# The adaLN modulation of a hybrid block by halves of the features, in plain fp32

## The chip, the cores and the metric

The kernel runs on one core of a Trainium2 chip. The metric is the time of one execution on the device, in microseconds. Before the change the median of three runs is 1171.71 us (1171.58 to 1171.74).

## The reference

One layer of a diffusion backbone, all in float32. A conditioning vector `c` and a learned vector `c_ctx` go through SiLU and a matrix `w_ada` [1024 x 6144]; the six sections of the result are shift, scale and gate for two sub-layers. The part at issue is the first use of shift and scale:

```python
mod_x = (silu_c @ w_ada[layer] + b_ada[layer])[:, None, :]
mod_c = silu_cc @ w_ada[layer] + b_ada[layer]
...
px = modulate(rms_norm(x, g_pre_mix[layer]), sh_m, sc_m) @ w_in[layer]
pc = modulate(rms_norm(ctx, g_pre_mix[layer]), csh_m, csc_m) @ w_in[layer]
```

`x` holds 1024 latent tokens and `ctx` 256 context tokens, of 1024 features each. `modulate(h, shift, scale)` is `h * (1 + scale) + shift`. The projections feed windowed attention and a bidirectional chunkwise mLSTM; an output projection and a SwiGLU sub-layer follow. Nothing can be projected before scale and shift are known, and every feature of a token enters each projected value.

## The kernel before

A float32 product of full accuracy is made of three matmuls of a rounded format (`mm3`, lines 77 to 79): each operand is split into a high part (a cast on ScalarE, ACT) and a low part (a subtraction on VectorE, DVE), and high x high, high x low and low x high are summed. A plain fp32 matmul does the same at once, in several passes.

**Head.** The DMA queue on SyncE (SP) takes the loads in a fixed order, each issued behind the one before (`issue_after(last)`). First come the modulation weights of the scale section (1) and the shift section (0), eight loads each of 128 rows x 1024 columns (`wa`, line 315, 512 KB, rows of 4 KB), with the first two token tiles between (`prep_a`, line 192). Six of the sixteen are multiplied in plain fp32 (`PLAIN`), ten are split (lines 65 and 66), and the stationary operand is the SiLU vector, four columns wide (`cz4`, `cs4`; products at line 334). The results `pr`, [4 x 512] twice per section, are copied to rows of `Vc` (ACT at line 355, DVE at 359), eight small transposes put them into columns (`pcol`, line 362), and DVE makes `scol` (scale and gain, lines 366 to 368) and `hcol` (shift, line 371), 128 partitions x 8 feature groups. `w1` (272 columns of `w_in`: gates, attention values and one mLSTM value head) is loaded behind and split at lines 295 and 300.

**Tokens.** There are ten tiles of 128 tokens, 0 to 7 latent and 8 and 9 context. For each of the tiles 0 to 5: load, sum of squares on ACT (line 196), root and reciprocal, scaling of the rows on GpSimd (POOL, line 204), eight transposes on TensorE (PE, line 220) into two PSUM tiles `pt`, one for each half of the features; then multiply by `scol` (line 243), add `hcol` (line 256, from tile 2 on on POOL), cast to the high part `hh` (line 268; 265 for tile 0) and subtract for the low part `hl` (line 269). Tiles 6 to 9 are loaded transposed and use the root as a row of factors. `s1(i)` is the slab of 272 columns: 24 matmuls over eight feature groups of 128 (for tile 0 in another order, lines 391 and 394). `s2(i)` is the slab of 384 columns, with weights `w2` split at lines 460 and 461. Three `s2` slabs (`NFILL = 3`) are put between the `s1` slabs; `gates()`, a chain of small steps on other engines, comes behind `s1(9)`, and the other seven `s2` slabs run on PE meanwhile. Then `tproj` makes 13 token projections (lines 608 to 611), and the rest of the layer follows.

The program is put in order by a scheduler that goes by data dependences and priority; `keep_in_program_order` (`pin` in the changed kernel) fixes an instruction's place among the others so marked, and `issue_after` holds an instruction behind another. Within an engine and within the load queue, instructions then run in the order of the list. Work buffers are `R(k, ...)`, sixteen of 4 KB per partition, where a later tile of the same number waits for the readers of the former.

## Time and profile before

| | |
|---|---|
| median of 3 runs | 1171.71 us (1171.58 to 1171.74) |
| the profiled execution's own time | 1171.69 us |
| its span | 1169.9 us |
| mean granted clock of TensorE | 0.998 |
| busy time | PE 1155.5 us (99%), DVE 782.8, ACT 558.6, POOL 154.5 |
| read from memory, written | 159.29 MB, 55.97 MB |

How to read it: times are from the span's start. A timeline row has start, length, engine, source line, operation, output<-input, tile, shapes, count, and in brackets the idle time before it with what ended it. A row of windows has the stretch, its length, busy time of PE, PE's weight loads, DVE, ACT and POOL with the count of instructions, the clock granted to PE (1.00 is full), the share in which the DMA engines were busy, and GB/s. Matmuls overlap, so the distance of two starts is the cost of one, not its length.

### The profile page before, as it was taken

What the parts mean: (1) busy time and instruction counts of PE and PEld (TensorE: products, weight loads), DVE (VectorE), ACT (ScalarE), POOL (GpSimd) and SP (SyncE); (2) the same over time, 40 slices, a digit from 0 to 9 for tenths busy, and PEclk for the clock granted to TensorE, in tenths of its full rate; (3) what the DMA queues carried; (4) which work ended last, traced back from release to release, by engine and by line L of the source; (5) the groups of instructions that cost most, each with busy time, mean ns of one, the idle gap of its engine ahead of it and who ended that gap; (6) DMA issues with size and microseconds to landing.
All of it is one profiled execution on the core that took longest, in us unless ns stands there. A gap on an engine that the chain in (4) does not pass through costs nothing.

```text
span 1169.9 us, 16222 instructions
## 1 busy us (share of the span) xinstructions
PE 1155.5 (99%) x5857; PEld 945.5 (81%) x5857; DVE 782.8 (67%) x1391; ACT 558.6 (48%) x1037; POOL 154.5 (13%) x201
## 2 busy tenths in 40 slices
PE   9899999999999999999999999999999999999997
PEld 3799888878888767888788888888888888888886
DVE  5874768873787643479777777767677755644557
ACT  6753442223777855877543333334343344434533
POOL 1430001263664630000000000000000000000000
PEclk9999999999999999999999999999999999999999
DMA  9722954657797605220334556566645467665853
GB/s 367 281 68 80 391 175 144 210 170 230 206 254 202 174 10 198 90 83 26 99 135 171 199 206 241 212 201 219 222 143 161 150 212 273 201 208 191 307 181 126
DMA packets 103272, 216.99 MB, mean 185 GB/s; under 512 B 10260, under 2 KB 39572, under 8 KB 101784
## 3 DMA queue, kind: packets, MB, share of 16 engines
q1 hardware_dynamic: 103192, 215.95, 55.5%
q8 instruction: 46, 0.75, 0.3%
q14 instruction: 34, 0.28, 0.1%
HBM read 159.29 MB, written 55.97 MB: 184 GB/s over the span
## 4 chain that ended last, share of the span: by engine, by line
PE 95%; DMA 2%; DVE 2%; issue 0%; ACT 0%; SPq 0%; DVEq 0%
PE xv L79 8%; PE xv L77 8%; PE xv L78 8%; PE pt L78 6%; PE pt L79 6%; PE pt L77 6%; PE t L609 4%; PE t L611 4%; PE t L608 4%; PE pt L1063 3%; PE pt L1045 3%; PE op L77 3%; PE op L78 3%; PE op L79 2%; PE fx L77 2%; PE fx L79 2%
## 5 line engine op out<-in xcount | busy, mean ns | idle before, releaser
L66 DVE TENSOR_TENSOR fo<-fr,fo 128x1024 fp32r<-128x1024 f32 x77 | 92.8, 1223 | 71.4 <-ACT fo L65 69.9
L65 ACT CAST fo<-fr 128x1024 fp32r<-128x1024 f32 x77 | 79.5, 1049 | 74.1 <-PE pt L79 38.2
L608 PE MATMUL t<-hh,th 128*128 128x512 f32 x208 | 82.4, 396 | 0.0
L609 PE MATMUL t<-hl,th 128*128 128x512 f32 x208 | 82.0, 394 | 0.0
L1445 ACT CAST wS<-wr 128x512 fp32r<-128x512 f32 x88 | 54.2, 622 | 55.4 <-PE pt L79 36.8
L1447 DVE TENSOR_TENSOR wS<-wr,wS 128x512 fp32r<-128x512 f32 x88 | 60.4, 689 | 19.7 <-ACT wS L1445 19.7
L79 PE MATMUL xv<-tT,wS 128*128 128x512 f32 x168 | 65.6, 391 | 0.0
L77 PE MATMUL xv<-tT,wS 128*128 128x512 f32 x168 | 65.6, 391 | 0.0
L78 PE MATMUL xv<-tT,wS 128*128 128x512 f32 x168 | 65.5, 390 | 0.0
L611 PE MATMUL t<-hh,tl 128*128 128x512 f32 x208 | 65.0, 393 | 0.0
L77 PE MATMUL op<-woh,mh 128*128 128x512 f32 x128 | 50.9, 397 | 0.0
L79 PE MATMUL op<-woh,ml 128*128 128x512 f32 x128 | 50.0, 390 | 0.0
L78 PE MATMUL op<-wol,mh 128*128 128x512 f32 x128 | 50.0, 390 | 0.0
L1193 DVE TENSOR_TENSOR wr<-wr 128x512 f32<-128x512 f32 x66 | 45.5, 690 | 1.4
L608 PEld LDWEIGHTS t<-hh,th 128*128 128x128 f32 x208 | 39.1, 188 | 8.3 <-issue 0.3
L1479 ACT ACTIVATE es<-es 128x512 f32<-128x512 f32 x22 | 13.9, 633 | 66.6 <-DVE es L1196 66.5
L609 PEld LDWEIGHTS t<-hl,th 128*128 128x128 f32 x208 | 39.1, 188 | 8.0 <-issue 1.2
L77 PE MATMUL pt<-fo 128*128 128x512 f32 x110 | 42.8, 389 | 0.0
L78 PE MATMUL pt<-fo 128*128 128x512 f32 x110 | 42.8, 389 | 0.0
L79 PE MATMUL pt<-fo 128*128 128x512 f32 x110 | 42.8, 389 | 0.0
L611 PEld LDWEIGHTS t<-hh,tl 128*128 128x128 f32 x208 | 37.2, 188 | 6.5 <-issue 0.3
L782 PE MATMUL s<-k,qh 128*128 128x256 f32 (+1 forms) x128 | 41.6, 336 | 0.5 <-DVE sm L784 0.5
(788 smaller groups left out, 3339.3 us busy)
## 6 DMA issues: line engine op xcount, KB each, us to landing
wr<-in_wfi SPq DMA_DIRECT2D x44, 512.0 KB, 5.2
wb<-in_wada SPq DMA_DIRECT2D x24, 512.0 KB, 5.8
s_d<-a SPq DMA_DIRECT2D x22, 512.0 KB, 6.7
bt<-in_wfo SPq DMA_DIRECT2D x44, 256.0 KB, 3.4
tb_d<-bt SPq DMA_DIRECT2D x11, 1024.0 KB, 3.9
fr<-s_d SPq DMA_DIRECT2D x44, 256.0 KB, 4.4
fr<-tb_d SPq DMA_DIRECT2D x44, 256.0 KB, 4.6
fr<-a_d SPq DMA_DIRECT2D x33, 256.0 KB, 4.3
```

The lines of the kernel that those rows point to most:

```text
L65: act.copy(hi, raw)
L66: dve.tensor_tensor(lo, raw, hi.bitcast(F32), SUB)
L77: pe.matmul(ps, a[0], b[0], start=first, stop=False, **kw)
L78: pe.matmul(ps, a[0], b[1], start=False, stop=False, **kw)
L79: pe.matmul(ps, a[1], b[0], start=False, stop=last, **kw)
L608: pe.matmul(o, wh[:, kt], m[0], start=f, stop=False)
L609: pe.matmul(o, wh[:, kt], m[1], start=False, stop=False)
L611: pe.matmul(o, wl[:, kt], m[0], start=False, stop=l)
L782: pe.matmul(o, qh[:, h, :], k2[g][:, kc], start=True, stop=False)
L1193: dve.tensor_tensor(out, a, b, SUB)
L1445: act.copy(w[:, 0], raw)
L1447: dve.tensor_tensor(w[:, 1], raw, w[:, 0].bitcast(F32), SUB)
```

## The change

- The modulation is worked out by halves of the features, 512 each, and both sections at once. `wa_load(h, kt)` brings, for 128 rows of `w_ada`, the 512 columns of half `h` of both sections, [128 x 2 x 512], 512 KB with rows of 2 KB. All eight loads of the first half come first, with token tile 0 among them; the eight of the second half come between `w1` and token tiles 1 to 3.
- All products are plain fp32, none is split. The stationary operand `cz` has 32 columns, of which two hold the SiLU vectors and 30 are zero. `pr_mm` puts its product into one of four groups of 32 columns of the array, by section and by even or odd `kt`, so that one PSUM bank holds four partial results. `mod_out(h)` copies the bank in two halves (ACT and DVE) and sums even and odd by four small products with a selector (`sel4`), which also puts the result into columns. DVE makes `hcol` and `scol` for the half.
- The slabs `s1` of tiles 0 to 3 are made in two halves of 12 matmuls, `s1_half(i, 0)` and `s1_half(i, 1)`, over the features of one half each. The four first halves stand between the products of the second modulation half; the four second halves stand behind its end. The second-half features of these tiles wait as unscaled copies in `hraw` (`early0`) and are scaled by DVE and ACT in `early1`. Tiles 1 to 5 add on DVE, not on POOL.
- `warm(n)` adds n small matmuls on PE whose result is not used.
- `NFILL` is 4: the fourth `s2` slab comes ahead of `s1(8)`, and six are left for the time of `gates()`. The order of `s1`, `s2` and the small products from tile 4 on is written out with `then`.

How the instructions stand, in three places. On PE, around the first slab. Before, the second section's products, tile 1's transposes between them, and all of the modulation's end (`pr` is the product's bank, `pcol` the columns):

```order
L334 MATMUL pr_211<-wa_2_239,cz_123 4x512
L334 MATMUL pr_212<-wa_2_239,cz_123 4x512
L220 MATMUL pt<-vec,xt_225 128x128 x8
L220 MATMUL pt<-vec,xt_232 128x128 x4
...
L334 MATMUL pr_211<-wa_7_269,cz_123 4x512
L334 MATMUL pr_212<-wa_7_269,cz_123 4x512
L334 MATMUL pr_211<-hl_104,cs_122 4x512
L334 MATMUL pr_212<-hl_104,cs_122 4x512
L362 MATMUL pcol<-vec,Vc 128x4 x8
L391 MATMUL slab<-w1h_117,hh_101 128x272
```

And now, where `pr_124` is the first half's bank and `pr_259` the second's:

```order
L355 MATMUL pr_124<-wa_7_194,cz 32x512 x2
L365 MATMUL warm<-ones,cz 32x128 x2
L382 MATMUL pcol_125<-st,Vc 128x4 x4
L365 MATMUL warm<-ones,cz 32x128 x3
L440 MATMUL slab<-w1h_117,hh_101 128x272
...
L442 MATMUL slab<-w1h_117,hl_103 128x272 x4
L355 MATMUL pr_259<-wa_0_203,cz 32x512 x2
L355 MATMUL pr_259<-wa_1_205,cz 32x512 x2
L365 MATMUL warm<-ones,cz 32x128 x2
L231 MATMUL pt<-vec,xt_200 128x128 x8
L355 MATMUL pr_259<-wa_2_210,cz 32x512 x2
L355 MATMUL pr_259<-wa_3_212,cz 32x512 x2
L448 MATMUL slab<-w1h_117,hh_101 128x272
```

The first slab now stands ahead of all products of the second half, and tile 1's transposes behind it. On the load queue (SP), the order before from the shift section on:

```order
L315 DMA wa_1_217<-in_wada 128x1024
L192 DMA xt_225<-in_x 128x1024
L192 DMA xt_232<-in_x 128x1024
L315 DMA wa_2_239<-in_wada 128x1024
...
L315 DMA wa_7_269<-in_wada 128x1024
L289 DMA wr_0_306<-in_ws 128x1088
L289 DMA wr_1_308<-in_ws 128x1088
```

And now, from the first half's last two loads on (`wr_0` and `wr_1` are `w1`, `xt` a token tile):

```order
L349 DMA wa_6_189<-in_wada 128x2x512
L349 DMA wa_7_194<-in_wada 128x2x512
L330 DMA wr_0_198<-in_ws 128x1088
L189 DMA xt_200<-in_x 128x1024
L349 DMA wa_0_203<-in_wada 128x2x512
L349 DMA wa_1_205<-in_wada 128x2x512
L189 DMA xt_207<-in_x 128x1024
...
L349 DMA wa_5_219<-in_wada 128x2x512
L330 DMA wr_1_221<-in_ws 128x1088
L349 DMA wa_6_223<-in_wada 128x2x512
L349 DMA wa_7_225<-in_wada 128x2x512
```

`wr_0` is the tenth transfer of this list behind the small first one, where it was the nineteenth. On DVE, behind the first half's columns, now (no such list stood there before; the splits of `wa` and whole-feature steps did):

```order
L386 TENSOR_TENSOR scol<-scol,st 128x2x4
L337 TENSOR_TENSOR w1l_119<-wr_0_198,w1h_117 128x2x272 x2
L236 TENSOR_TENSOR hraw_158<-pt,scol 128x512
L240 TENSOR_TENSOR hraw_158<-hraw_158,hcol 128x512
L256 TENSOR_TENSOR hl_103<-hraw_158,hh_101 128x4x128
L208 RECIPROCAL st<-st 128x1 x2
L236 TENSOR_TENSOR hraw_202<-pt,scol 128x512
L240 TENSOR_TENSOR hraw_202<-hraw_202,hcol 128x512
L256 TENSOR_TENSOR hl_103<-hraw_202,hh_101 128x4x128
```

Each tile has one multiply, one add and one low part here, of its first half alone, and the reciprocals of tiles 1 and 2 stand ahead of tile 1's multiply.

The diff, cut to the modulation, the half slabs and the order that is written out:

```diff
-    q1.tile([P, 64], F32, name="padw")
-    cs4 = q1.tile([P, KT, 4], F32R, name="cs4")
-    cz4 = q1.tile([P, KT, 4], F32, name="cz4")
-    split(cs4[:, :, 0:2], cs4[:, :, 2:4], csil)
-    pool.memset(cz4, 0.0)
-    dve.tensor_copy(cz4[:, :, 0:2], csil)
+    cz = q1.tile([P, KT, 32], F32, name="cz")
+    pool.memset(cz, 0.0)
+    dve.tensor_copy(cz[:, :, 0:2], csil)
...
+    XT, NE = 6, 4
+    pin = tc.keep_in_program_order
+    def prep_l(i):
         j = i - NT
         xt = xts[i] = R(4 + i % 4, f"xt{i}", (D,))
         xd[i] = dma(xt, x[i * P:(i + 1) * P] if i < NT else ctx[j * P:(j + 1) * P])
+        hraw[i] = R((2, 3, 8, 9, 10, 11, 12, 13, 8, 9)[i], f"hraw{i}", (KT, P))
         if i >= XT:
+            with tc.issue_after(w2d[1]):
+                dma(hraw[i], xtr[i - XT])
+        return xd[i].ins
+    def prep_c(i, parts=(0, 1)):
+        xt, r = xts[i], st[:, 10 + i:11 + i]
+        if 0 in parts:
+            q = act.activation(xt if i >= XT else hraw[i].rearrange("p a b -> p (a b)"), xt, AF.Square,
+                               accum_out=st[:, i:i + 1])
+            if i:
+                pin(q)
+            q = act.activation(r, st[:, i:i + 1], AF.Sqrt, bias=epst, scale=1.0 / D)
+            if i:
+                pin(q)
+        if 1 in parts:
+            q = dve.reciprocal(r, r)
+            if 0 < i <= XT:
+                pin(q)
+            if i < XT:
+                pool.tensor_scalar(xt, xt, r, 1.0, MUL, MUL)
...
+    def h_mul(o, a_, q, b, e=dve):
+        return e.tensor_tensor(o, a_, hcast(scol[:, q, 4 * b:4 * b + 4]), MUL)
+    def h_add(r, q, b, e):
+        return e.tensor_tensor(r, r, hcast(hcol[:, q, 4 * b:4 * b + 4]), ADD)
+    def h_act(o, a_, b):
+        for k in range(4):
+            kk = 4 * b + k
+            pin(act.activation(o[:, k], a_[:, k], AF.Identity, scale=scol[:, 0, kk:kk + 1], bias=hcol[:, 0, kk:kk + 1]))
+    def h_dve(o, a_, b):
+        for k in range(4):
+            kk = 4 * b + k
+            pin(dve.tensor_scalar(o[:, k], a_[:, k], scol[:, 0, kk:kk + 1], hcol[:, 0, kk:kk + 1], MUL, ADD))
+    def low(i, b, r):
+        q = dve.tensor_tensor(hl[b][:, :, i * P:(i + 1) * P], r, hh[b][:, :, i * P:(i + 1) * P].bitcast(F32), SUB)
+        return pin(q) if i < NE else q
+    def high(i, b):
+        return hh[b][:, :, i * P:(i + 1) * P]
+    def early0(i, fill=None):
+        if i:
             prep_t(i)
+            if fill:
+                fill()
+        pin(act.copy(rw(i, 1), pts[i][1]))
+        if i:
+            pin(h_mul(rw(i, 0), pts[i][0], 0, 0))
+            pin(h_add(rw(i, 0), 0, 0, dve))
+            pin(act.copy(high(i, 0), rw(i, 0)))
+            low(i, 0, rw(i, 0))
+    def early1():
+        h_act(high(0, 1), rw(0, 1), 1)
+        h_dve(rw(0, 0), rw(0, 1), 1)
+        prep_c(4, (1,))
+        h_dve(rw(1, 1), rw(1, 1), 1)
+        pin(act.copy(high(1, 1), rw(1, 1)))
+        prep_c(5, (0,))
+        low(0, 1, rw(0, 0))
+        h_dve(rw(2, 1), rw(2, 1), 1)
+        pin(act.copy(high(2, 1), rw(2, 1)))
+        low(1, 1, rw(1, 1))
+        h_dve(rw(3, 1), rw(3, 1), 1)
+        prep_c(5, (1,))
+        pin(act.copy(high(3, 1), rw(3, 1)))
+        low(2, 1, rw(2, 1))
+        low(3, 1, rw(3, 1))
...
-    PLAIN = {1: (0, 2, 4), 0: (0, 2, 7)}
-    last, nsp, late = None, 0, []
-    for sec in (1, 0):
-        pr = [pa.tile([4, 512], F32, name=f"pr{sec}{i}", tag="mm", bufs=4) for i in range(2)]
-        for kt in range(KT):
-            w = R(8 + kt, f"wa{sec}_{kt}", (D,))
-            with tc.issue_after(last) if last is not None else ExitStack():
-                last = dma(w, wada[kt * P:(kt + 1) * P, sec * D:(sec + 1) * D]).ins
-            if kt in PLAIN[sec]:
-                ops = ((cz4, w),)
-            else:
-                wh, wl = (t[1 - nsp // 4 % 2][:, nsp % 4] for t in (hh, hl))
-                nsp += 1
-                split(wh, wl, w)
-                ops = ((cs4, wh), (cs4, wl))
...
+    last, was, prs_, pcols = None, {}, {}, {}
+    def chain(f, *z):
+        nonlocal last
+        with tc.issue_after(last) if last is not None else ExitStack():
+            last = f(*z)
+    def wa_load(h, kt):
+        w = was[h, kt] = R(8 + kt if not h else 10 + kt % 6, f"wa{h}_{kt}", (2, 512))
+        return dma(w, wada[kt * P:(kt + 1) * P, 0:2 * D].rearrange("p (s c) -> p s c", s=2)[:, :, 512 * h:512 * h + 512]).ins
+    def pr_mm(h, *kts):
+        for kt in kts:
+            for i in range(2):
+                g = 32 * (2 * (kt % 2) + i)
+                pin(pe.matmul(prs_[h][g:g + 32], cz[:, kt, :], was[h, kt][:, i], start=kt < 2, stop=kt > 5))
+    prs_[0] = pa.tile([P, 512], F32, name="pr0", tag="mm", bufs=4)
+    pcols[0] = pa.tile([P, 4, 4], F32, name="pcol0", tag="gx", bufs=2)
+    wm = pa.tile([P, 4, P], F32, name="warm", tag="gx", bufs=2)
+    def warm(n):
+        for i in range(n):
+            pin(pe.matmul(wm[0:32, i % 4], cz[:, 0, :], ones, start=True, stop=True))
+    sel4 = st[:, 32:36]
+    gsb = st[:, 36:44]
+    for i in range(2):
+        dve.tensor_tensor(sel4[:, 2 * i:2 * i + 2], ident[:, 32 * i:32 * i + 2], ident[:, 64 + 32 * i:66 + 32 * i], ADD)
+    dve.scalar_tensor_tensor(gsb, bcol(1), 1.0, vec[:, VGPM:VGPM + 8], ADD, MUL)
+    def both(t):
+        return t.rearrange("p (o k) -> p o k", o=1).broadcast_to([P, 2, 4])
+    def mod_out(h):
+        rr = Vc.rearrange("p n h v -> p (n h v)")[:, 512 * h:512 * h + 512]
+        f = slice(4 * h, 4 * h + 4)
+        pin(act.copy(rr[:, 0:256], prs_[h][:, 0:256]))
+        pin(dve.tensor_copy(rr[:, 256:512], prs_[h][:, 256:512]))
+        for k in range(4):
+            pin(pe.matmul(pcols[h][:, k, :], rr[:, k * P:(k + 1) * P], sel4, start=True, stop=True))
+        pv_ = pcols[h].rearrange("p k (i q) -> p i q k", q=2)
+        pin(dve.tensor_tensor(hcol[:, :, f], pv_[:, 0], both(bcol(0)[:, f]), ADD))
+        pin(dve.tensor_tensor(scol[:, :, f], pv_[:, 1], both(vec[:, VGPM + 4 * h:VGPM + 4 * h + 4]), MUL))
+        pin(dve.tensor_tensor(scol[:, :, f], scol[:, :, f], both(gsb[:, f]), ADD))
+    for kt in range(KT):
+        chain(wa_load, 0, kt)
+        pr_mm(0, kt)
+        if kt < KT - 1:
+            warm(1)
+        if kt == 2:
+            chain(prep_l, 0)
+            prep_c(0)
+        if kt == 5:
+            prep_t(0)
+            early0(0)
+    for f in ((w1_load, 0), (prep_l, 1), (wa_load, 1, 0), (wa_load, 1, 1), (prep_l, 2), (wa_load, 1, 2), (wa_load, 1, 3),
+              (prep_l, 3), (wa_load, 1, 4), (wa_load, 1, 5), (w1_load, 1), (wa_load, 1, 6), (wa_load, 1, 7), (prep_l, 4),
+              (lambda: dma(bcr, bcast(bcv)).ins,), (prep_l, 5)):
+        chain(*f)
+    warm(2)
+    mod_out(0)
+    warm(3)
+    w1_split(0)
+    h_act(high(0, 0), pts[0][0], 0)
+    pin(h_mul(rw(0, 0), pts[0][0], 0, 0))
+    pin(h_add(rw(0, 0), 0, 0, dve))
+    low(0, 0, rw(0, 0))
...
+    s1ps = {}
+    def s1_half(i, b, mid=None):
+        if not b:
+            s1ps[i] = pa.tile([P, 512], F32, name="slab", tag="mm", bufs=4)
+        o = s1ps[i][:, :272]
+        if not i or b:
+            for k in range(4):
+                for w in (w1h, w1l):
+                    pin(pe.matmul(o, hop(i, 4 * b + k)[0], w[b][:, k], start=not b and not k and w is w1h, stop=False))
+            for k in range(4):
+                pin(pe.matmul(o, hop(i, 4 * b + k)[1], w1h[b][:, k], start=False, stop=b == 1 and k == 3))
+        else:
+            for k in range(4):
+                if mid and k == 2:
+                    mid()
+                h_, l_ = hop(i, k)
+                pin(pe.matmul(o, h_, w1h[0][:, k], start=not k, stop=False))
+                pin(pe.matmul(o, h_, w1l[0][:, k], start=False, stop=False))
+                pin(pe.matmul(o, l_, w1h[0][:, k], start=False, stop=False))
+        if b:
+            s1_out(i, s1ps.pop(i))
...
-    NFILL = 3
+    NFILL = 4
...
+    prs_[1] = pa.tile([P, 512], F32, name="pr1", tag="gx", bufs=2)
+    s1_half(0, 0)
+    pr_mm(1, 0, 1)
+    warm(2)
+    prep_c(1)
+    prep_c(2)
+    early0(1, lambda: pr_mm(1, 2, 3))
+    s1_half(1, 0)
+    prep_c(3)
+    early0(2, lambda: pr_mm(1, 4, 5))
+    s1_half(2, 0)
+    w1_split(1)
+    warm(2)
+    early0(3, lambda: pr_mm(1, 6, 7))
+    pcols[1] = pa.tile([P, 4, 4], F32, name="pcol1", tag="gx", bufs=2)
+    s1_half(3, 0, lambda: mod_out(1))
+    pool.memset(Vc[:, :, :, 128:129], 1.0)
+    prep_c(4, (0,))
+    early1()
+    s1_half(0, 1)
+    prep_t(4)
+    s1_half(1, 1)
+    prep_b(4)
+    s1_half(2, 1)
+    chain(lambda: dma(cst, const).ins)
+    for b in range(2):
+        for k in (0, 2):
+            raw = w2r[b, k] = R((14 if not b else 0) + k // 2, f"wr384_{b}{k}", (2, 384))
+            chain(lambda: dma(raw, ws2[:, b, k:k + 2]).ins)
+            w2d[b] = last
+    s1_half(3, 1)
+    prep_t(5)
+    prep_b(5)
+    def prep_d(i):
+        with tc.issue_after(w2d[1]):
+            prep_l(i)
+        prep_c(i)
+    seq = None
+    def then(f, i):
+        nonlocal seq
+        with tc.issue_after(seq) if seq is not None else ExitStack():
+            seq = f(i)
+    prep_d(6)
...
+    then(s1, 4)
+    for m_, c_ in ((mF, up), (mB, lw)):
+        pin(dve.tensor_scalar(m_, c_, -1.0, -NEG, ADD, MUL))
+    prep_d(7)
+    then(s1, 5)
+    then(prep_t, 6)
+    prep_b(6)
+    prep_d(8)
+    then(s2, 0)
+    then(prep_t, 7)
+    prep_b(7)
+    then(s2, 1)
+    then(s1, 6)
+    prep_d(9)
+    then(prep_t, 8)
+    prep_b(8)
+    then(s2, 2)
+    then(s1, 7)
+    then(prep_t, 9)
+    prep_b(9)
+    then(s2, 3)
+    then(s1, 8)
+    then(s1, 9)
```

More of the change, by code (lines that the diff above doesn't have):

```diff
@@ L78, in mm3 @@
         pe.matmul(ps, a[0], b[1], start=False, stop=False, **kw)
-        pe.matmul(ps, a[1], b[0], start=False, stop=last, **kw)
+        return pe.matmul(ps, a[1], b[0], start=False, stop=last, **kw)
     def bcast(ap_row, n=P):
@@ L213, in prep_t @@
             pts[i] = pa.tile([P, 4, P], F32, name="pt", tag="tp", bufs=2)[:, 0]
-            pe.matmul(pts[i], st[:, 10 + i:11 + i].broadcast_to([P, P]), ident, start=True, stop=True)
-            return
-        for b in parts:
-            pt = pa.tile([P, 4, P], F32, name="pt", tag="tp" if i else "mm", bufs=2 if i else 4)
+            return pe.matmul(pts[i], st[:, 10 + i:11 + i].broadcast_to([P, P]), ident, start=True, stop=True).ins
+        for b in range(2):
+            pt = pa.tile([P, 4, P], F32, name="pt", tag="tp", bufs=2)
@@ L253, in prep_b @@
         tok = slice(j * P, (j + 1) * P)
[L254 to L277 removed]
+        if i >= XT:
+            r = hraw[i]
+            for k in range(KT):
+                dve.scalar_tensor_tensor(r[:, k], r[:, k], scol[:, q, k:k + 1], pts[i], MUL, MUL)
+            for b in range(2):
+                h_add(rw(i, b), q, b, pool)
+        if i < XT:
+            h_act(rw(i, 1), pts[i][1], 1)
+            pin(h_mul(rw(i, 0), pts[i][0], q, 0))
+            pin(h_add(rw(i, 0), q, 0, dve))
+        for b in range(2) if i >= XT else (1, 0):
+            h_ = hs[b][:, :, tok]
+            pin(act.copy(h_, rw(i, b)))
+            r = dve.tensor_tensor(ls[b][:, :, tok], rw(i, b), h_.bitcast(F32), SUB)
+            if i < XT:
+                pin(r)
     def slab_load(hi, lo, src, n, k0):
@@ L289, in w1_load @@
         return dma(w1r[i], ws1[:, i]).ins
-    def w1_split(i, part=None):
-        if part is None or -1 in part:
-            for k in (0, 2):
-                r = act.copy(w1h[i][:, k:k + 2], w1r[i][:, k:k + 2])
-                if part:
-                    tc.keep_in_program_order(r)
-        for k in (0, 1) if part is None else part if part[0] >= 0 else ():
-            sl = slice(2 * k, 2 * k + 2)
-            r = dve.tensor_tensor(w1l[i][:, sl], w1r[i][:, sl], w1h[i][:, sl].bitcast(F32), SUB)
-            if part:
-                tc.keep_in_program_order(r)
@@ L304, in body, with w1_split @@
-    PLAIN = {1: (0, 2, 4), 0: (0, 2, 7)}
-    last, nsp, late = None, 0, []
-    wm = pa.tile([P, 4, P], F32, name="warm", tag="mm", bufs=4)
+    def w1_split(i):
+        for k in (0, 2):
+            pin(act.copy(w1h[i][:, k:k + 2], w1r[i][:, k:k + 2]))
+        for k in (0, 2):
+            pin(dve.tensor_tensor(w1l[i][:, k:k + 2], w1r[i][:, k:k + 2], w1h[i][:, k:k + 2].bitcast(F32), SUB))
+    last, was, prs_, pcols = None, {}, {}, {}
[3 more added lines that the diff above has]
+            last = f(*z)
@@ L415, in body @@
     NI = NT + NC_
-    NFILL = 3
-    w2h, w2l, s2ps = [], [], {}
+    NFILL = 4
+    w2h, w2l, s2ps, w2r = [], [], {}, {}
     def s2(i, bs=(0, 1)):
@@ new lines, in body @@
+    seq = None
[4 more added lines that the diff above has]
+    prep_d(6)
+    wc = None
+    for b in range(2):
+        w2h.append(w2_tile("h", b, f"w2h_{b}").rearrange("p (k n) -> p k n", k=4))
+        w2l.append(w2_tile("l", b, f"w2l_{b}").rearrange("p (k n) -> p k n", k=4))
+        for k in (0, 2):
+            with tc.issue_after(wc) if wc is not None else ExitStack():
+                wc = pin(act.copy(w2h[b][:, k:k + 2], w2r[b, k])).ins
+            dve.tensor_tensor(w2l[b][:, k:k + 2], w2r[b, k], w2h[b][:, k:k + 2].bitcast(F32), SUB)
@@ new lines, in body @@
+    ch += [R(i, f"ch{i}", (4, L), F32R) for i in range(2)]
+    cl += [R(2 + i, f"cl{i}", (4, L), F32R) for i in range(2)]
+    then(s1, 4)
[17 more added lines that the diff above has]
+    then(prep_t, 9)
```

182 lines of the change are left out of this document (19 added, 163 removed).

## The prediction

> **What bounds the kernel now.** I read the chain of waits first, then TensorE's timeline, then windows over single stages. The chain over the first 200 us, start and length in us:
>
> ```profile
> 1.66 4.96 DMA wa<-in_wada
> 9.34 8.96 DMA xt<-in_x
> 18.32 11.56 DMA wr<-in_ws
> 29.90 0.66 ACT w1h L295
> 30.58 1.36 DVE w1l L300 x2
> 31.94 0.60 DVE Vc L359
> 33.43 0.47 ACT hh L265
> 33.94 3.73 PE slab L391 x16
> ```
>
> Until 29.9 us the chain is loads, one behind the other: 16 modulation weights, two token tiles, then `w1`. Then come four short steps, and from 33.94 PE carries it. The page says what follows:
>
> ```profile
> PE 95%; DMA 2%; DVE 2%; issue 0%; ACT 0%; SPq 0%; DVEq 0%
> ```
>
> So time can be won only ahead of or between the first slabs. TensorE's timeline gives the sizes:
>
> ```profile
> 5.46 1.88 PE L334 MATMUL pr<-wa,cz 128*4 128x512 f32 x4
> ...
> 33.94 0.39 PE L391 MATMUL slab<-w1h,hh 128*128 128x272 f32 x1 [0.95 <-ACT hh L265]
> ...
> 39.10 1.04 PE L220 MATMUL pt<-vec,xt 128*128 128x128 f32 x8
> 39.90 0.37 PE L77 MATMUL slab<-w1h,hh 128*128 128x272 f32 x1
> ...
> 44.92 0.39 PE L79 MATMUL slab<-w1h,hl 128*128 128x272 f32 x1 [1.45 <-DVE hl L269]
> ...
> 81.11 0.34 PE L77 MATMUL slab<-w2h,hh 128*128 128x384 f32 x1
> ...
> 83.20 0.28 PE L77 MATMUL slab<-w1h,ch 128*128 128x272 f32 x1
> ...
> 86.21 0.34 PE L77 MATMUL slab<-w2h,hh 128*128 128x384 f32 x1
> ...
> 118.26 0.39 PE L608 MATMUL t<-hh,th 128*128 128x512 f32 x1
> ```
>
> Eight transposes take 0.80 (39.10 to 39.90). A 272-column slab of 24 matmuls takes 3.01 (83.20 to 86.21). Half a 384-column slab takes 2.09, a whole one 4.18. The token projections start at 118.26; seven 384-column slabs lie between 86.21 and there, so the gates and the rest take 32.05 - 29.26 = 2.8. Between 33.94 and 118.26 lie 84.3 us: ten small slabs 30.1, ten large ones 41.8, transposes of tiles 2 to 5 3.2, four small products for tiles 6 to 9 0.6 (estimate), gates 2.8, together 78.5, so 5.8 us is waiting or slow clock.
>
> **The sum has one figure: when do the token projections start?** From there the order on PE is the same but for a few shifted small products, and PE is the chain.
>
> **Loads.** The queue now brings the same 16 x 512 KB, but the first slab needs the first ten transfers (eight half loads, a token tile, half of `w1`) and not the first twenty. A half load has rows of 2 KB in place of 4 KB. Three windows bound its pace (length; busy time of PE, PEld, DVE, ACT, POOL; clock; DMA share; GB/s):
>
> ```profile
> 4.00:28.00 24.00, 22.61 (x90) 7.42 (x89) 14.55 (x21) 15.21 (x24) 2.24 (x2) 1.00 1.02 408
> 1080.00:1100.00 20.00, 20.00 (x90) 16.57 (x89) 8.58 (x7) 6.96 (x8) 0.00 (x0) 1.00 0.99 373
> 1000.00:1060.00 60.00, 60.00 (x267) 49.69 (x266) 31.58 (x30) 25.61 (x31) 0.00 (x0) 1.00 0.62 192
> ```
>
> Now it is 408 GB/s, 1.28 us for 512 KB. The second window holds weight loads with 2 KB rows and saturated queues: 373 GB/s, 1.41 us. The third, of such loads too, moved 192 at a share of 0.62, so 310 GB/s or 1.69 us at worst. I take 1.41, since that window is saturated as this one will be. The first load is there at 5.4 (first product 5.46), so the eighth half at 5.4 + 7 x 1.41 + 1.28 = 16.6, and the last second half, 13 transfers on (eight halves, two `w1` of 1.36, three token tiles), at 34.4.
>
> **Modulation products.** Removed are ten splits with their products; added are 32 plain fp32 products of 32 columns in four column groups. Two products of a pair with unlike columns are in the trace once:
>
> ```profile
> 307.87 0.60 PE L1045 MATMUL pt<-vec,pr__2716 128*128 128x128 f32 x4
> 308.40 0.64 PE L1063 MATMUL pt<-ts__3048,av 128*64 128x512 f32 x1
> 308.40 0.64 PE L1063 MATMUL pt<-ts__2895,av 128*64 128x512 f32 x1
> 308.88 0.59 PE L1063 MATMUL pt<-ts__3048,av 128*64 128x512 f32 x1
> ...
> 310.60 0.59 PE L1063 MATMUL pt<-ts__2857,av 128*64 128x512 f32 x1
> 311.12 0.45 PE L782 MATMUL s<-k,qh 128*128 128x384 f32 x1
> ```
>
> They start together and come 0.43 apart, two passes each, so a pair takes 0.86, where two plain products one after another took 1.88 (row at 5.46). For the first half a pair waits for each load: 0.86. For the second half four go together; four at once are not shown, so the bounds are 0.86 and 1.72. I take 0.86, which is how the groups of two behave, and keep 0.5 us of the end for the other (below).
>
> **The first slab.** Pair done 17.5; half-row copy 0.4 (256 columns, estimate from the 0.60 of 512 in the chain); four products with the selector 0.5 (estimate) and three small column operations 0.5: scale and shift at 19.3, where the step that reads them began at 33.4. On ACT the `w1` casts (two of 0.66) stand ahead of tile 0's features, which adds until 20.2; one of 0.47 more, and the first slab starts at 20.7. That is 13.2 earlier.
>
> **What is pushed behind that start.** Tile 1's transposes 0.8, four groups of second-half products 3.4, four fillers 0.8 (0.21 each, an estimate: a quarter of the plain 512-row product's 0.94, half of 1.88, and a little overlap), the second selector 0.5: 5.5 us of PE work that lay before the first slab, now behind it.
>
> **More waiting.** Here the groups count (min/median/max ns of one):
>
> ```profile
> L243 DVE TENSOR_TENSOR hraw<-pt,scol x11: 668/679/685, 24.8 to 56.9; 128x512 f32<-128x512 f32 x11
> L256 DVE TENSOR_TENSOR hraw<-hraw,hcol x4: 673/683/686, 33.6 to 37.9; 128x512 f32<-128x512 f32 x4
> L269 DVE TENSOR_TENSOR hl<-hraw,hh x16: 668/690/1532, 36.1 to 70.9; 128x512 fp32r<-128x512 f32 x16
> L268 ACT CAST hh<-hraw x15: 602/620/628, 34.8 to 70.2; 128x512 fp32r<-128x512 f32 x15
> L196 ACT ACTIVATE hraw<-xt x6: 1040/1052/1077, 19.3 to 43.8; 128x1024 f32<-128x1024 f32 x6
> L204 POOL TENSOR_SCALAR xt<-xt,st x4: 1117/1124/1434, 21.1 to 50.9; 128x1024 f32<-128x1024 f32 x4
> ```
>
> Tiles 1 to 3 each need transposes, multiply 0.68, add 0.68, cast 0.62, subtract 0.69 before their half slab of 1.5 ends. On ACT two squares (1.05 and the read of the sum, 1.25) are queued ahead of tile 1's copy and cast; on DVE both reciprocals stand ahead of its multiply. Stepping the queues by hand with these durations, PE has 13.2 us of work between 20.7 and 39.8, when the first second half-slab can go; it waits 5.9 us there. The last loads land at 34.4, when the 34.5 transposes of tile 3 only begin, so they are not what is late: the engines are. From 39.8 to the end of the slab of tile 4 at 52.9 lie 10.65 us of PE work and 2.4 of waiting, for low parts on DVE. Of these 1.2 come from two rows, VectorE's subtract held while GpSimd scales:
>
> ```profile
> 43.22 1.11 POOL L446 TENSOR_SCALAR xt<-xt,st 128x1024 f32<-128x1024 f32 x1
> 43.34 1.53 DVE L269 TENSOR_TENSOR hl<-hraw,hh 128x512 fp32r<-128x512 f32 x1
> ```
>
> (0.69 otherwise.) Later 0.5: from 52.9 PE runs five small slabs, ten large ones, gates and small products, 60.2 with it, and the projections start at 113.6. Waiting is 8.8 in all against 5.8, so 3.0 more; of the fourth large slab that moves ahead of the gates nothing is gained or lost, since six large slabs of 4.18 still cover the gates' steps. The splits saved on ACT and DVE ran beside the loads: nothing for them.
>
> **Sum:** 13.2 - 5.5 - 3.0 = 4.7 us, less roundings 4.6 (118.26 to 113.6).
>
> **Less two.** The clock first (the rows' clock column):
>
> ```profile
> 32.03:35.44 3.41, 2.06 (x15) 1.57 (x14) 2.84 (x9) 2.79 (x8) 0.11 (x1) 1.00 1.04 410
> 35.44:38.85 3.41, 3.41 (x16) 3.36 (x16) 3.17 (x7) 2.74 (x6) 0.00 (x0) 0.50 1.02 403
> 42.27:45.68 3.41, 1.96 (x16) 1.73 (x15) 2.35 (x5) 2.82 (x8) 2.57 (x3) 1.00 0.26 106
> 45.68:49.10 3.42, 3.42 (x32) 3.42 (x31) 2.56 (x4) 2.98 (x7) 1.83 (x2) 1.00 0.72 171
> ```
>
> After a stretch with 2.06 us of busy PE the next ran at half clock (0.50); after one of 1.96 it did not (1.00). Busy time alone does not decide it, then, but it tips somewhere near that share. My stretches around 18.4 to 21.8 (1.9) and 25.2 to 28.6 (1.7) are at or below both. The existing dip is gone, which is in the 5.8; a new one costs between nothing (over a wait) and 2.0 (both stretches' followers). I take 1.0. The Trainium skill (TensorE: Matmul & The Clock Gate, "Why this matters for your kernels") sets the bar at a gap of about 3 us between bursts; this trace differs, as its longest gap before the half clock was 0.95. By that rule no dip would come, and the sum at the end would be 4.1 instead of 3.1.
>
> Second, going into column groups and out. At 308.27 four transposes are through (four at 0.10), the pair starts at 308.40, its first pass takes 0.05 more, and after 311.03 the next starts at 311.12: 0.27 per visit. Five visits behind the first slab make 1.35 at most; most fall where PE waits anyway, I take 0.5. The Trainium skill (TensorEngine Tiling (Array Packing), "Key Properties") says that changing the tiling mode drains the engine; the 0.27 agrees, and by the rule with nothing hidden the whole 1.35 would count, 0.85 more than I charge.
>
> 4.6 - 1.0 - 0.5 = 3.1, and 1171.69 (the profiled execution, 0.02 below the median of the runs) gives **1168.6 us**.
>
> **Rivals.** (a) Column groups run one after the other: each pair 1.88, each four 3.8. The eighth pair then ends at 21.4 instead of 17.5, the second-half groups add 10 us at places where the next tile stands behind them, and the stepped end is 4.7 later than before: **1176.4**, slower. The rows at 308.40 speak against it for two groups; it decides if 32-column groups of one bank are not independent. Chance 0.06. (b) PE held at half clock from 20 us on: small slab matmuls are 0.213 apart (16 in the 3.41 us from 35.44) instead of 0.125 (24 in 3.01). Held until 42 the steps give 1.2 later than before, until 50 3.1: with the 0.5 for the visits **1173 to 1175**. It decides if each stretch up to there stays under the bar; the fillers speak against, the two thin stretches for. Chance 0.12. (c) Half loads at 1.69: the end moves 3.3 and 1.3 of the 4.6 stays, less the two charges: **1170.9 to 1171.9**, no change; or the gain is used up in waits that I don't see (`w2` casts, gates). The third window speaks for it, the second against. Chance 0.22. (d) Loads at 1.28 (1.2 more), no held subtract (1.2 more), no dip: **1164.6 to 1166**. Chance 0.10. (e) Mine, 1167 to 1169.8: 0.50.
>
> **How the numbers follow.** The bar of what can be told from no change is 0.2%, 2.3 us: faster below 1169.4, slower above 1174.05. Faster: (d) 0.10, nearly all of (e) 0.47, a little of (c) 0.05: 0.62. Slower: (a) 0.06, half of (b) 0.06, and 0.03 for what I have not thought of: 0.15. The rest, 0.23, the same. The range goes from (d)'s 1164.6 to 1174.0 inside (b), which leaves out (a), part of (b) and what beats (d). The likeliest case's own is 1167 to 1169.8.
>
> **What would show it.** First slab at 20.7, give or take 1 (1.28 loads: 19.6; groups in turn: 24). Pairs of the second half starting together. PE's waits between 21 and 40 at about 6 us, for `hh` and `hl`, not for `wa`. Clock 0.50 in at most two stretches before 40. Tile 4's slab ended by 53 to 54, projections from 114 to 116, and the rest as long as before: 1171.69 - 118.26. I am wrong if that rest changes by over 1 us, or if PE waits for `wa` past 22.

## The result: slower, 1175.88 us against 1171.72

The changed kernel took 1175.88 us (median of 6 executions, 1175.43 to 1177.23), the kernel before, beside it, 1171.72 (6, 1171.58 to 1173.46): a ratio of 1.0035 with an interval of 1.0022 to 1.0048. The forecast was 1168.6, the range ended at 1174.0. The profiled execution took 1177.23 us at a mean clock of 0.995 and is the slowest of the six; its span is 1175.5. The others took up to 1176.66, and four of them had 0.997 or 0.998. What follows is read from the profiled executions.

The span is longer by 5.6 us, and two instructions divide it: the first token projection (`t`) and the first attention score (`s`). Of before, TensorE's timeline has the second one at:

```profile
283.70 0.38 PE L782 MATMUL s<-k,qh 128*128 128x256 f32 x1
```

And TensorE's timeline of the changed kernel, from the first slab on:

```profile
19.88 0.39 PE L440 MATMUL slab<-w1h,hh 128*128 128x272 f32 x1 [0.25 <-ACT hh L246]
...
23.11 1.27 PE L442 MATMUL slab<-w1h,hl 128*128 128x272 f32 x4 [1.25 <-DVE hl L256]
24.31 1.94 PE L355 MATMUL pr<-wa,cz 128*32 128x512 f32 x8
...
27.01 1.19 PE L231 MATMUL pt<-vec,xt 128*128 128x128 f32 x8
28.13 1.07 PE L355 MATMUL pr<-wa,cz 128*32 128x512 f32 x8
29.92 0.39 PE L448 MATMUL slab<-w1h,hh 128*128 128x272 f32 x1 [0.73 <-ACT hh L277]
...
43.65 0.39 PE L440 MATMUL slab<-w1h,hh 128*128 128x272 f32 x1 [0.20 <-ACT hh L246]
...
46.68 0.77 PE L442 MATMUL slab<-w1h,hl 128*128 128x272 f32 x4 [1.37 <-DVE hl L256]
...
54.97 0.39 PE L79 MATMUL slab<-w1h,hl 128*128 128x272 f32 x1 [1.00 <-DVE hl L316]
...
118.35 0.39 PE L707 MATMUL t<-hh,th 128*128 128x512 f32 x1
...
172.21 0.33 PE L810 MATMUL pk<-vec,mkc 128*128 128x128 f32 x1 [0.89 <-ACT mkc L729]
173.48 0.66 PE L816 MATMUL pu<-Vc,mkc 128*64 128x129 f32 x8 [0.95 <-DVE mkc L812]
...
288.93 0.38 PE L881 MATMUL s<-k,qh 128*128 128x256 f32 x1
```

Up to the projections the head has won nothing: 118.35 against 118.26, though its first slab starts 14.1 us earlier (19.88 against 33.94). From the projections to the first score it takes 170.58 us (288.93 - 118.35) where before took 165.44 (283.70 - 118.26): 5.1 us lost in a stretch that the change does not touch. Behind that the two differ by 0.4. In what follows the first number is called the start, the second the stretch.

In the stretch stand two waits at 172 us that before did not have, for `mkc`, the convolved keys of the mLSTM's context part, and two shorter ones for it later, 1.1 together. The list of all that TensorE waited for (us in total, times, longest) has them among its first:

```profile
PE slab L442 <- DVE hl L256: 2.6, 2, 1.4
PE slab L448 <- ACT hh L277: 2.2, 3, 0.7
PE pu L816 <- DVE mkc L812: 2.0, 3, 0.9
...
PE pk L810 <- ACT mkc L729: 0.9, 1, 0.9
```

And the windows around the two places (length; busy time of PE, PEld, DVE, ACT, POOL; clock; DMA share; GB/s):

```profile
16.84:20.25 3.41, 2.69 (x24) 2.06 (x19) 1.74 (x6) 2.34 (x6) 0.00 (x0) 1.00 1.03 392
20.25:23.66 3.41, 2.16 (x10) 1.84 (x9) 2.51 (x5) 1.96 (x5) 0.44 (x1) 0.53 1.04 391
23.66:27.08 3.42, 3.42 (x17) 1.38 (x16) 0.16 (x1) 1.45 (x3) 1.71 (x2) 0.50 1.04 396
...
43.50:47.50 4.00, 2.49 (x14) 2.01 (x15) 4.00 (x13) 2.69 (x6) 1.25 (x1) 1.00 0.41 159
...
172.05:175.46 3.41, 2.31 (x14) 1.75 (x15) 3.41 (x6) 1.07 (x3) 0.00 (x0) 0.79 0.33 85
175.46:178.87 3.41, 3.41 (x12) 2.73 (x11) 1.49 (x4) 1.18 (x3) 2.39 (x1) 0.71 0.36 112
```

The clock fell twice: to half in the head, over two windows, and to 0.79 and 0.71 from the waits at 172 on. Over 160 to 205 us it is 0.96, which is 1.8 us; with the 2.9 of waits for `mkc` that is 4.7 of the 5.1. From 43.5 to 47.5 it is DVE that has no idle time.

Why `mkc` is late stands on other engines. First the rows of before, from the load queue (SPq) and ACT:

```profile
106.40 0.33 SPq L521 DMA_DIRECT2D a_d<-g  x1
...
140.72 0.33 SPq L551 DMA_DIRECT2D w_dr<-w  x1
...
150.80 0.42 ACT L630 ACTIVATE mkc<-ct 128x256 f32<-128x256 f32 x1 [4.00 <-DVE ct L629]
```

Then those of the changed kernel:

```profile
110.65 0.33 SPq L620 DMA_DIRECT2D a_d<-g  x1
...
150.23 2.95 SPq L757 DMA_DIRECT2D wb<-in_wada  x5
153.36 0.45 SPq L650 DMA_DIRECT2D w_dr<-w  x1
...
163.20 1.28 ACT L729 ACT_TABLE_LOAD   x1 [2.40 <-DMA w_dr<-w]
164.50 0.42 ACT L729 ACTIVATE mkc<-ct 128x256 f32<-128x256 f32 x1
```

`a_d` is the store at the end of the chain that `gates()` begins; behind it the eight weight tiles `w` of the mLSTM are made (loaded, summed, exponentiated on ACT, stored to `w_dr`). The fourth large slab stands ahead of `s1(8)` now, so the gates begin one slab later: 110.65 in place of 106.40, 4.25 us, with the projections at the same time. The delay grows on the way. The last of the eight stores was issued at 140.72 before; now it is issued at 153.36, 12.6 later, right behind the tile's exponential, which ends on ACT at 153.33 (140.69 before). It stands behind five loads of 512 KB (`wb`) and lands 9.8 us after its issue, near 163.2, where the last store before took 7.6. What share of the growth from 4.25 to 12.6 each step of these lists makes was not varied. It matters because `mkc` is buffer 8 of `R`, and the last weight tile (n = 7, entry 7 % 5 = 2 of the table `(6, 7, 8, 15, 5)`) is buffer 8 too: ACT may not write the one before the store of the other has been read out, and it waits 2.40 for that (row at 163.20). Ahead of it in ACT's list stands the cast of the next weights, which had waited 6.42 for TensorE. The first `mkc` comes 13.7 us later than before, and the second 13.0 later, at 171.74 in place of 158.70: it is ready at 172.15, and TensorE would take it right behind its product at 171.05.

### The profile page after: what moved, and what is told of

It reads as the page before. It is cut to its first block, busy times and chain, and to the rows that moved or that the text cites. A ratio compares the mean times of both kernels' runs of the same rounds, so it can differ in the third digit from the quotient of the medians.

```text
span 1175.5 us, 16268 instructions
## 1 busy us (share of the span) xinstructions
PE 1154.2 (98%) x5889; PEld 948.2 (81%) x5889; DVE 768.4 (65%) x1392; ACT 554.6 (47%) x1038; POOL 140.3 (12%) x194
## 4 chain that ended last, share of the span: by engine, by line
PE 89%; DVE 6%; DMA 2%; issue 1%; ACT 1%; POOL 1%; SPq 0%; DVEq 0%; ACTq 0%; POOLq 0%
PE xv L79 8%; PE xv L77 8%; PE xv L78 8%; PE pt L79 6%; PE pt L77 6%; PE pt L78 6%; PE pt L1162 3%; PE pt L1144 3%; PE op L77 2%; PE op L78 2%; PE op L79 2%; PE t L708 2%; PE t L707 2%; PE t L710 2%; PE slab L77 2%; PE fx L77 2%
```

## The experiments

Two theories stand against each other here. The one: the loss lies behind the projections, and the fourth large slab ahead of the gates makes it, by way of the late stores and the shared buffer. The other: the loss lies in the head, in the clock and in the short steps of ACT and DVE, and the waits at 172 cost little. A kernel that takes away one link at a time tells them apart.

### Three large slabs ahead of the gates, as before

```diff
-    NFILL = 4
+    NFILL = 3
...
-    then(s2, 3)
     then(s1, 8)
...
     for i in range(NFILL, NI):
-        s2(i)
+        if i == NFILL:
+            then(s2, i)
+        else:
+            s2(i)
```

> The changed kernel with three large slabs ahead of the gates as before (NFILL = 3, the fourth held behind s1 of tile 9). Theory A (the fourth slab ahead of the gates brings the gates' chain 4.2 us nearer to the token projections, the mLSTM weights behind it come late, and PE then waits for mkc near 172 us): projections still start at 118.3, no wait for mkc, 1171 to 1172.5 us. Rival B (the stall comes from the new head as such, whatever NFILL is): 1175 to 1177 us, with the wait near 172 still there.

Measured: 1173.06 us (11 executions, 1170.87 to 1174.67), ratio to before 1.0008 (1.0000 to 1.0017), a little above what theory A expected. The two rows that divide the span:

```profile
120.55 0.39 PE L709 MATMUL t<-hh,th 128*128 128x512 f32 x1
...
285.99 0.39 PE L883 MATMUL s<-k,qh 128*128 128x256 f32 x1
```

The stretch is 285.99 - 120.55 = 165.44, exactly before's, and TensorE has no wait for `mkc` left. ACT still waits for the last store here, 2.08 us, but the two `mkc` are written at 154.20 and 161.15, early enough. So the number of slabs ahead of the gates makes the whole 5.1. The head, with the rest of the change in it, is no gain: its start is 2.3 later than before's here, with the clock at 0.93 from 20 to 45 us and 0.87 from 45 to 58.

### The kernel before, with four slabs ahead

```diff
-    NFILL = 3
+    NFILL = 4
...
-        if 3 <= i < 3 + 2 * NFILL:
+        if 3 <= i < 9:
             s2((i - 3) // 2, ((i - 3) % 2,))
+        if i == 8:
+            s2(3)
```

> The kernel before, with nothing changed but that the fourth large slab stands ahead of s1 of tile 8 (NFILL = 4). Theory A: the projections start at 118.3 as before and the waits for mkc near 172 us appear; 1175 to 1177 us. Rival B: no such wait, 1171.5 to 1172 us.

Measured: 1175.69 us (7 executions, 1174.39 to 1177.45), ratio 1.0031 (1.0020 to 1.0042): this one step, alone, makes the kernel before as slow as the changed one. Its rows of the load queue, of the waits and of a window:

```profile
110.72 0.33 SPq L523 DMA_DIRECT2D a_d<-g  x1
...
154.62 0.33 SPq L553 DMA_DIRECT2D w_dr<-w  x1
```

```profile
PE pu L719 <- DVE mkc L715: 0.9, 1, 0.9
PE pk L713 <- ACT mkc L632: 0.9, 1, 0.9
```

```profile
160.00:205.00 45.00, 43.17 (x218) 34.77 (x217) 34.54 (x45) 19.26 (x28) 5.92 (x10) 0.96 0.42 129
```

The start is before's, 118.42; `a_d` is late by the same 4.3; the last store is issued at 154.62; the stretch is 287.64 - 118.42 = 169.2, 3.8 more. Of these 1.8 are the two waits, and a clock of 0.96 over 45 us is 1.8 more. The clock falls only from 182 us on, to 0.70 and 0.80 in two windows of 3.41 us. Whether the waits bring that about is not shown: the kernel with nine more fillers, below, has the same two waits, a full clock behind them, and a stretch 3.0 longer than before's.

### Another buffer for the last weight tile

The least edit that leaves the fourth slab where it is, and the store as late as it is: two entries of the table change places, so that tile 7 lies in buffer 6.

```diff
-        wt_ = R((6, 7, 8, 15, 5)[n % 5], f"w{n}", (2, 4, P))
+        wt_ = R((8, 7, 6, 15, 5)[n % 5], f"w{n}", (2, 4, P))
```

> The changed kernel, where only the buffers of the mLSTM weight tiles rotate in another order ((8, 7, 6, 15, 5) for (6, 7, 8, 15, 5)), so that tile 7 no longer lies in the buffer that mkc takes over. If the last link of theory A is that mkc waits until weight tile 7 is stored (a store queued behind modulation loads): the wait near 172 us goes, 1171.5 to 1173 us. If it is only that exponentials and scalings come late on ACT and DVE: 1174.5 to 1177 us.

Measured: 1173.08 us (11 executions, 1170.01 to 1173.44), ratio 1.0005 (0.9996 to 1.0014). Its rows on TensorE, on ACT and on the load queue:

```profile
119.50 0.39 PE L707 MATMUL t<-hh,th 128*128 128x512 f32 x1
...
284.90 0.38 PE L881 MATMUL s<-k,qh 128*128 128x256 f32 x1
```

```profile
155.75 0.42 ACT L729 ACTIVATE mkc<-ct 128x256 f32<-128x256 f32 x1
```

```profile
158.66 0.33 SPq L650 DMA_DIRECT2D w_dr<-w  x1
```

`mkc` is written 2.9 us before that store is even issued, TensorE does not wait for it, and the stretch is 284.90 - 119.50 = 165.4. The chain is shown to its last link: the store may be late, if nothing has to wait for its buffer. What is left of the change, with a start of 119.50 here and 118.35 there, is no difference from before.

### More fillers around the first slab

The other half of the question is the head. Here the tail is left as in the changed kernel, and nine more fillers (the matmuls of `warm`) are to keep the clock up: four where two stood ahead of `mod_out(0)`, four where three stood behind it, and six in the first slab, between its high and its low part, where TensorE waited 1.25.

```diff
-    warm(2)
+    warm(4)
     mod_out(0)
-    warm(3)
+    warm(4)
...
+            if not i and not b:
+                warm(6)
```

> The changed kernel with 9 more filler matmuls: two ahead of the first half's selector products, one behind them, six between the high and the low part of tile 0's first half slab. Theory C (the half clock from 20.3 to 27.1 us costs 2.3 of the 4.7 us that the head came short of the steps): full clock throughout, tile 1's transposes at 24.7 instead of 27.0, projections at 116, and 1173 to 1174 us if the later stall stays the same size. Rival D (PE stands in engine chains there anyway, and fillers only take its time): clock better or not, projections at 118.0 to 119.5, 1175.5 to 1177 us.

Measured: 1177.51 us (5 executions, 1173.48 to 1178.46), ratio 1.0040 (1.0027 to 1.0054). The profiled one is the 1173.48, with a mean clock of 0.999; the others had 0.994 to 0.996. In the profiled one the clock was full through the head:

```profile
20.00:45.00 25.00, 20.72 (x142) 13.96 (x141) 15.12 (x34) 13.66 (x29) 4.73 (x5) 1.00 1.03 392
```

```profile
24.94 1.09 PE L231 MATMUL pt<-vec,xt 128*128 128x128 f32 x8
...
52.93 0.40 PE L79 MATMUL slab<-w1h,hl 128*128 128x272 f32 x1 [1.01 <-DVE hl L316]
...
116.32 0.39 PE L709 MATMUL t<-hh,th 128*128 128x512 f32 x1
```

Tile 1's transposes come 2.1 earlier than in the changed kernel (27.01), tile 4's slab 2.0 earlier (54.97), the projections 2.0. That is the price of the half clock in the head, where it comes, less what the nine fillers themselves cost. The profiled execution came out as theory C had it, but it is the fastest of the five by 2.8 us. The other four lost clock somewhere, where is not recorded, and the median is no better than the changed kernel's. The tail's loss was still there: a stretch of 168.5, 3.0 more than before's, at a full clock.

### The buffer, a shorter chain on DVE, and more fillers

Here the buffer is changed, tile 0's second low part is put ahead of tile 1's scaling on DVE (46.68 above had waited 1.37 for it), tiles 4 and 5 make their high parts in the order in which the slab reads them, and 24 more fillers than the change has fill the head up.

```diff
         prep_c(4, (1,))
+        low(0, 1, rw(0, 0))
         h_dve(rw(1, 1), rw(1, 1), 1)
...
-        low(0, 1, rw(0, 0))
...
-        for b in range(2) if i >= XT else (1, 0):
+        for b in range(2):
...
-            warm(1)
+            warm((1, 2, 6, 2, 1, 1, 1)[kt])
...
+    warm(2)
     s1_half(1, 0)
...
+    warm(3)
     s1_half(2, 0)
...
+    warm(3)
     pcols[1] = pa.tile([P, 4, 4], F32, name="pcol1", tag="gx", bufs=2)
```

(With the fillers and the table of the two kernels above.)

> The changed kernel with the other rotation of the weight buffers, with two moves in the head (tile 0's second low part straight behind its features on DVE, ahead of tile 1's; the low part of the first half ahead of the second for tiles 4 and 5) and with 22 more filler matmuls wherever PE waited between 7 and 41 us. Theory C (half clock in the head costs 2 us or more in most executions, and enough fillers keep it away): clock 1.00 to 45 us, projections at 114 to 115, 1167 to 1168.5 us. Rival D (fillers do not decide the clock, or delay the chains as much as they save): as without them, 1170 to 1172.5 us, with the mean clock near 0.996.

Measured: 1174.32 us (9 executions, 1173.79 to 1175.71), ratio 1.0023 (1.0014 to 1.0033): outside both ranges. The clock was 1.00 from 6 us to 118 and the stretch 165.4, and yet the start was 120.69. The longest entry of TensorE's waits ahead of it says why:

```profile
PE slab L78 <- DVE w2l L542: 2.9, 3, 1.4
```

These are the low parts of the large slab's weights `w2`, which the scheduler now put behind the scaling of tile 6 on DVE, and their casts behind the square of tile 7 on ACT, since the moves had changed what stood ready when. A gain in one chain was lost to an order that the program does not write out.

### The same moves with the fillers of the changed kernel

```diff
-            warm((1, 2, 6, 2, 1, 1, 1)[kt])
+            warm(1)
...
-    warm(4)
+    warm(2)
     mod_out(0)
-    warm(4)
+    warm(3)
...
-            if not i and not b:
-                warm(6)
...
```

(Against the kernel above; its other three calls of `warm` are taken out too.)

> The same rotation and the two moves in the head, with the fillers of the changed kernel only. The moves should take 1.2 (low part of tile 0) and 0.5 to 0.7 us (tile 4) off the waits ahead of the projections: 1.5 to 2 us less than with the rotation alone, 1171 to 1171.7 us. If PE only waits elsewhere then: 1172.5 to 1173.2 us. Against the run with more fillers it is the test of the clock: theory C 3 us or more above it, rival D equal.

Measured: 1176.05 us (5 executions, 1175.24 to 1176.25), ratio 1.0033 (1.0020 to 1.0046). The start is 122.87, the clock from 20 to 45 is 0.86, and the wait for `w2l` is there as well (2.5 in all). The time is above both ranges. Beside the kernel above it is 1.7 in the medians and 2.2 in the start: what the added fillers were worth there, between theory C (3 or more) and rival D (none).

### No fillers at all

The kernel with the other buffer, and every call of `warm` that the change added taken out.

```diff
-        if kt < KT - 1:
-            warm(1)
...
-    warm(2)
     mod_out(0)
-    warm(3)
...
-    warm(2)
...
```

> The changed kernel with the other rotation and without any filler behind the eleven at the start. Theory C: half clock for more of the stretch from 10 to 45 us than with the fillers (mean clock 0.993 to 0.995), 1174 to 1177 us. Rival D: 1172 to 1173 us, as the fillers' own 3 us of PE lay under waits.

Measured: 1172.17 us (11 executions, 1170.57 to 1172.54), ratio 0.9999 (0.9990 to 1.0008), beside 1173.08 for the same with fillers; the start is 118.62, although the clock is 0.88 from 6 to 20 us and 0.80 from 20 to 45 (0.99 and 0.87 with fillers). The fillers of the change bring nothing, then: they take time of their own (six, of two passes each, take 1.50 in the kernel with nine more) and did not keep the clock full. That part of what the half clock costs lies where TensorE waits for ACT and DVE anyway fits this, but is not shown by itself.

### The order of the weights written out, with many fillers and with none

The kernel with the moves and 24 more fillers, and two edges more: tile 7 is prepared behind the last cast of `w2`, tile 6 scaled behind its last low part.

```diff
-            dve.tensor_tensor(w2l[b][:, k:k + 2], w2r[b, k], w2h[b][:, k:k + 2].bitcast(F32), SUB)
+            wl_ = dve.tensor_tensor(w2l[b][:, k:k + 2], w2r[b, k], w2h[b][:, k:k + 2].bitcast(F32), SUB).ins
...
-    prep_d(7)
+    with tc.issue_after(wc):
+        prep_d(7)
...
-    prep_b(6)
+    with tc.issue_after(wl_):
+        prep_b(6)
```

> As the run with rotation, two moves and 22 more fillers, and now tile 7's square on ACT and tile 6's scaling on DVE are held behind the splits of the large slabs' weights (w2), which in that run had come late. If the wait for w2 low parts (2.9 us) was what ate the gain of the moves: no wait for w2l, projections at 116 to 118 instead of 120.7, 1169.5 to 1171.5 us. If PE then waits for tiles 6 and 7 instead: 1172.5 us or more.

Measured: 1170.90 us (11 executions, 1170.48 to 1171.61), ratio 0.9987 (0.9978 to 0.9995): a little faster than before, 0.9 us, and the fastest of all. The second of the two is the same without any filler:

> The same with no filler at all behind the first eleven: against the run just above it is the test of fillers and clock, with all else alike. Theory C (half clock sets the head): 2 to 4 us above it, 1172.5 to 1174 us. Rival D (the head is set by the chains of ACT, DVE and POOL, the fillers' PE time weighs as much as the half clock): within 1 us of it or below, 1169.5 to 1171.5 us.

Measured: 1171.57 us (11 executions, 1171.24 to 1172.14), ratio 0.9995 (0.9986 to 1.0004). The two windows of the head, first with fillers, then without:

```profile
20.00:45.00 25.00, 22.47 (x158) 15.82 (x158) 14.49 (x30) 12.90 (x28) 4.60 (x5) 1.00 1.03 394
```

```profile
20.00:45.00 25.00, 20.77 (x121) 14.33 (x120) 13.82 (x29) 12.82 (x28) 4.59 (x5) 0.80 1.03 393
```

A full clock against 0.80 over 25 us, and the starts are 117.58 and 117.88. With the order mended, the fillers and a full clock win 0.3 us of the start and 0.7 of the time, as rival D had it. In this order the clock hardly moves the end of the head; with the same buffer and moves but without the written order, fillers and a full clock had moved it by 2.2 (122.87 and 120.69).

All starts and stretches together, each from the profiled execution (the kernel before has 118.26, 165.44 and 1171.69):

| kernel | start | stretch | profiled execution, us | median, us | ratio |
|---|---|---|---|---|---|
| the change | 118.35 | 170.58 | 1177.23 | 1175.88 | 1.0035 |
| three slabs ahead | 120.55 | 165.44 | 1174.03 | 1173.06 | 1.0008 |
| before, four ahead | 118.42 | 169.22 | 1175.69 | 1175.69 | 1.0031 |
| other buffer | 119.50 | 165.40 | 1173.01 | 1173.08 | 1.0005 |
| nine more fillers | 116.32 | 168.47 | 1173.48 | 1177.51 | 1.0040 |
| buffer, moves, 24 more fillers | 120.69 | 165.40 | 1174.17 | 1174.32 | 1.0023 |
| buffer, moves | 122.87 | 165.39 | 1176.25 | 1176.05 | 1.0033 |
| buffer, no fillers | 118.62 | 165.40 | 1172.17 | 1172.17 | 0.9999 |
| buffer, moves, order, 24 more fillers | 117.58 | 165.40 | 1171.06 | 1170.90 | 0.9987 |
| buffer, moves, order, no fillers | 117.88 | 165.39 | 1171.31 | 1171.57 | 0.9995 |

The stretch is 165.4 wherever TensorE does not wait for `mkc`, and 168.5 to 170.6 where it does.

## Why the prediction was wrong, point by point

**The step that failed** is the sentence that of the fourth large slab, moved ahead of the gates, "nothing is gained or lost", with its last form, "the rest as long as before". It asked whether TensorE has cover for the gates' own steps, found six large slabs, and was right in that: TensorE is busy without a gap from 58 to 118 us. It did not ask what is late next. Moving 4.2 us of TensorE's work ahead of `s1(8)` keeps TensorE's own sum as it was, and pushes the start of a chain on SP, DVE and ACT 4.25 us back against it; that chain goes on for 50 us, past the projections' start, and ended on a shared buffer. Rows of the trace before point at it: the last store at 140.72, landed 7.6 later at 148.3, five 512 KB loads from 150.77 on, and `mkc` at 150.80 in the buffer of the stored tile, 2.5 us behind the landing. TensorE took the second `mkc`, ready at 159.1, at about 171, so 12 us of slack were left there. The 4.25 alone would not have used both up (an estimate from these rows); the 12.6 of the last store, and its landing behind the loads, did. The prediction had named the right observation to look for, a rest that changes by over 1 us, and priced it at nothing.

**The first slab** was predicted at 20.7, give or take 1, and came at 19.88. The load term was too careful: the windows show 391 to 396 GB/s, about 1.33 us for 512 KB where 1.41 was taken (408 and 1.28 before), so rows of 2 KB cost nearly nothing here, and rival (c) falls as far as it is about loads. Its other half, a gain that is used up in waits I did not see, with the gates among the places, is what came, but it ended at 1171.9 and so priced a used-up gain and no loss.

**Column groups:** four go together. The four products at 28.13, of two passes each (x8), take 1.07, where two such products, one after the other, took 1.88 before. Rival (a) falls, and so does the upper bound of 1.72.

**The clock:** one dip at 1.0 was charged, and one of two windows came, which cost 2.0 (the start of the changed kernel against that with nine more fillers at a full clock, 118.35 - 116.32). The size was off by 1.0. The rule behind the charge, a bar near 2 us of busy time in a stretch of 3.41, is not borne out: half clock followed a stretch with 2.69 busy (from 16.84), and none followed one with 2.04 (from 44.14). It is rival (b)'s place, but it was over by 27 and not held to 42.

**The steps from the first slab to the projections** are the second term that was mis-sized. Of the head's 4.7 us over the stepped 113.6, the first slab gives back 0.8, the clock takes 2.0, and 3.5 are left, of which 0.5 was charged for going into column groups. They are not waits: the prediction had 8.8 us of waiting from the first slab on, and TensorE stood idle for 6.6 (91.85 busy of the 98.47 from 19.88 to 118.35). Too small was the work, 84.1 stepped (13.2, 10.65 and 60.2): of the 91.85, two windows at half clock make 3.3, which leaves 88.5. Most of the excess lies ahead of 43.65, where the second halves begin: 19.52 busy, 16.2 without the half clock, against 13.2. The rows show where: four products take 1.07 and not 0.86, eight transposes 0.97 and 1.02 from start to start (at 32.00 and 37.49) and not 0.80, the columns (`pcol`) 0.80 and not 0.5, and the first matmul behind a wait stands 0.23 ahead of the next, not 0.125. The prediction's base has the same error. Its 5.8 of "waiting or slow clock" before the change hold 1.9 of idle time (82.45 busy of 84.32) and 1.7 of half clock; the other 2.2 are work that the sum had too small.

The chain of waits shows that the engines take turns (start, length):

```profile
27.80 0.70 DVE hraw L236
28.52 0.70 DVE hraw L240
29.25 0.63 ACT hh L277
29.90 0.70 DVE hl L256
30.65 0.39 PE slab L450
```

From a tile's multiply to the product that reads its low part are 2.85 us, three times, where the four rows of the prediction add up to 2.67; TensorE can cover the time of its second-half products alone. Then `h_dve`, four operations of a quarter each, which the prediction does not price:

```profile
43.10 1.12 DVE hraw L252 x4
44.28 0.17 issue
44.44 1.58 DVE hraw L252 x3
46.02 0.61 DVE hl L256
```

They take 0.28 apiece and 1.12 for the four, where one row for all four quarters, with a tensor as its second operand, takes 0.68. The second such group, from 44.20 on, takes 1.82 while POOL scales (1.25 from 44.45). That an operation would be held there was in the sum, though placed on the subtracts. In the four microseconds from 43.5 DVE has no idle time (4.00 of 4.00 in the window above). All this is read from one trace; no run varied one of these steps alone, so how the 3.5 divides among them stays open.

**The sum again, with what was measured:** 1171.69 for before's profiled execution, 0.1 for the start, 5.1 for the stretch and 0.4 behind it make 1177.3; its like of the changed kernel took 1177.23. From the forecast's side, 1168.6 had the start at 115.1 (113.6 and 1.5 charged): 3.2 of the miss lie in the head, 5.1 in the stretch. Without the shared buffer the result would have been about no difference, which is what 1173.08 shows: inside the range, but not the gain that was forecast.
